# Two heads' matmuls issued in turn, and 512-column accumulators for z and the convolution, in a hybrid attention and state-space block

## The chip, the core and the metric

The kernel runs on one core of a Trainium2 chip. TensorE (PE) multiplies, its weight loads are listed apart (PEld); VectorE (DVE), ScalarE (ACT) and GpSimd (POOL) do the elementwise work, SyncE (SP) issues most transfers. Times are device microseconds (us) of one execution. Everything is float32; the large products run in float32r, a form that TensorE takes in one pass, and the small ones in plain float32, which stands in the trace as two weight loads and two matmuls for each matmul of the program.

## What is computed

A decoder block over 256 positions with 2048 channels: a modulated RMS norm, one wide input projection, a sparse attention branch and a Mamba-2 branch from it, a gated merge, and a SwiGLU feed-forward. Cut to the parts that the change touches:

```python
proj = h @ w_in
c_q, c_kv, k_idx, w_idx, z, xbc, dt_raw, g_a, g_b = jnp.split(proj, split_points, axis=-1)
...
# lightning indexer, 16 heads of 64, for two blocks of 128 queries
idx_score = jnp.einsum('bqh,bqhs->bqs', wi,
                       jax.nn.relu(jnp.einsum('bqhd,bsd->bqhs', qi, k_idx)))
...
# Mamba-2: depthwise convolution over 6144 channels, then chunks of 128 positions
conv = lax.conv_general_dilated(xbc, conv_w[:, None, :], ...)
conv = jax.nn.silu(conv + conv_b)
...
y_intra = jnp.einsum('btsgh,bsghp->btghp', w, xq)
y_inter = jnp.einsum('btgn,bghpn->btghp', cq, state) * jnp.exp(a_cs)[..., None]
...
y = y.reshape(B, L, D_INNER) * jax.nn.silu(z)
```

z has 4096 channels and xbc 6144.

## The kernel before

**Products in three terms.** Channels lie on the partitions, the 256 positions on the columns. Each weight tile of 128x128 is split into a rounded part wh (ACT, line 155) and a rest wl (DVE, line 156), and each moving operand is a 512-column tile: columns 0 to 255 its rounded part, 256 to 511 its rest. A product is wh times both halves plus wl times the rounded half. `mm3` (line 177) writes it in one of two forms, by the accumulator's width. With 256 columns it issues three matmuls of 256 columns (lines 182 to 184) into one sum. With 512 columns it issues one matmul of 512 columns (line 179) and one of 256 (line 180); then the two halves of the accumulator still have to be added, which `evac` (line 220) does: ACT copies the upper half to SBUF (line 223), DVE adds the lower half to it (line 224). A weight tile and what mm3 does with it is called a block below; a job is 16 blocks, one piece of 1 MB of weights.

**Who uses which.** Before the change the wide form is used by the projections pa, out, gu and dn, and the narrow form by the first part of the input projection (acc_s), by iq, by z (acc_z, 32 jobs), by the convolution's input (acc_cv, 48 jobs) and by pb. acc_s, acc_z, acc_cv and acc_gu have h as moving operand (gu's is a second tile h2 in the same place, with the same tag of a pool of one buffer); pb has y, pa has o, dn has ffact.

**What follows a z job.** `add_z` (line 686): ACT takes the tanh out of the accumulator (line 689), DVE forms (tanh + 1) times the accumulator (line 690), and the result goes to DRAM. **What follows a convolution job.** `conv_post` (line 811): ACT copies the accumulator to u (line 827) and makes the first tap from it (line 831), DVE adds three taps (line 833), ACT takes the tanh (834), DVE multiplies (836). After six such jobs `ssd_gen` runs the recurrence of one of eight groups, spread over the following jobs' blocks.

**The two-head matmuls.** In `ssd_gen` (lines 915 to 928) four tiles py of a group each take two heads, the first on output partitions 0 to 63, the second on 64 to 127. Each head has three float32 matmuls of 128 contraction rows, 64 output partitions and 128 columns (lines 922, 923, 924), so a py tile has six in the program and twelve in the trace. In `index_gen` (line 572) each of 16 heads has 64 contraction rows, even heads on partitions 0 to 63, odd ones on 64 to 127, each with its own accumulator; two matmuls a head (lines 580, 581).

**Order.** The kernel is written as a list of jobs. Their weights are loaded ahead on SP's queue, and a job's split is called two jobs before its matmuls (AHEAD = 2, three buffers each for wh and wl). What follows a product is deferred to the next job, and generators advance at set blocks of a job. Every engine takes its instructions in the order in which the framework's scheduler put them down; NACC = 4 accumulators are in turn.

Of the kernel before, what the change touches and what calls it, by code (L numbers as in the profile page):

```python
# [9 lines left out]
F32 = mybir.dt.float32  # L10
# [6 lines left out]
P = 128  # L17
# [26 lines left out]
def hybrid_block_kernel(  # L44
# [43 lines left out]
    def ps_side(name):  # L88
        return pss.tile([P, 512], F32, tag="ps", name=name)
# [326 lines left out]
    def full(key, src, post, **kw):  # L416
        product_jobs(key, [src], [(0, k) for k in range(KT)], hr, lambda m, acc: post(acc), **kw)
# [155 lines left out]
    def index_gen():  # L573
        t = A["t"]
        sc, kT, wi = A["sc"], A["kT"], A["wi"]
        for hd in range(NH):
            q = A["qi"][(hd % 2) * 64 : (hd % 2) * 64 + 64, hd // 2]
            kk = kT[(hd % 2) * 64 : (hd % 2) * 64 + 64]
            ps = ps_side(f"ix{hd}")
            pe.matmul(ps[:, 0:128], q[:, 0:128], kk[:, 0:128], start=True, stop=True)  # L580
            pe.matmul(ps[:, 128:384], q[:, 128:256], kk, start=True, stop=True)
# [104 lines left out]
    def add_z(j, ticks=1):  # L686
        def post(acc):
            th = tmp.tile([P, L], F32, tag="zt", name="zt")
            act.activation(th, acc, AF.Tanh, scale=0.5)
            dve.scalar_tensor_tensor(th, th, 1.0, acc, op0=ALU.add, op1=ALU.mult)  # L690
            nc.sync.dma_start(d_z[j], th)

        full(f"z{j}", w_z[j], post, ticks=ticks)
# [119 lines left out]
    def conv_post(g, i):  # L813
# [3 lines left out]
        def post(acc):  # L817
# [9 lines left out]
            act.activation(u[:, 3:], acc, AF.Copy)  # L827
# [3 lines left out]
            act.activation(c, acc, AF.Identity, scale=w(3), bias=cc[:, C_CB + j : C_CB + j + 1])  # L831
# [10 lines left out]
    def ssd_gen(g, xc, bc, ar):  # L842
# [72 lines left out]
        for j in range(4):  # L915
            z = load_z(j)
            py = ps_side("py")
            for i in range(2):
                hd = 2 * j + i
                o = py[64 * i : 64 * i + 64]  # L920
                xs = slice(64 * hd, 64 * hd + 64)
                pe.matmul(o[:, 0:128], xd[:, 0, xs], dd[:, hd, 0:128], start=True, stop=True)
                pe.matmul(o[:, 128:256], xd[:, 1, xs], dd[:, hd, 128:256], start=True, stop=False)
                pe.matmul(o[:, 128:256], st[:, xs], cd[:, hd], start=False, stop=True)
            if prev:
                finish(*prev)
            prev = (j, py, z)
            yield
# [21 lines left out]
    def add_conv(g, i, pre=None):  # L950
        full(f"cv{g}_{i}", w_ssm[6 * g + i], conv_post(g, i), pre=pre, ticks=3)
# [361 lines left out]
```

## Time and profile before

| | us |
|---|---|
| median of 3 runs | 2071.28 |
| lowest and highest | 2068.83, 2073.79 |
| the profiled execution, its own time | 2073.97 |
| its span, first to last instruction | 2072.0 |

The page says how long each engine was busy, and which chain of work ended last. Matmuls overlap in the trace (a matmul's record lasts some 280 ns while the next begins after 120), so PE's busy share hides small gaps; how fast PE goes is read from the starts of matmuls that follow each other.

### The profile page before, as it was taken

To read this page: it belongs to the slowest core of one execution; us is meant where nothing else is said; L and a number is where in the kernel's file an instruction comes from. 1 tells how busy PE (TensorE), PEld (TensorE's weight loads), DVE (VectorE), ACT (ScalarE), POOL (GpSimd) and SP (SyncE) were. 2 spreads that over 40 slices of the span, in tenths; PEclk is the share of its full clock that TensorE was granted. 3 is DMA by queue.
4 is the path that set the end of the run, shared out by engine and by line. 5 is a ranking of instruction groups with operands and counts; after the bars stand their busy time and mean duration, and the time that the engine had idled before them with its cause. 6 is when DMAs were issued, how large, how long until landed. Compare 5 with 4: busy or idle time off the path is not lost.

```text
span 2072.0 us, 34189 instructions
## 1 busy us (share of the span) xinstructions
PE 2003.7 (97%) x14116; PEld 1858.8 (90%) x14116; DVE 1462.3 (71%) x1779; ACT 1018.0 (49%) x1408; POOL 257.4 (12%) x216
## 2 busy tenths in 40 slices
PE   2999999999999999999999999999999999999997
PEld 2999999999899999999999978788888888888886
DVE  7799778866778887778777855667776555544443
ACT  3544654564354665566663444444444444443442
POOL 4043200310000111110112334000000000000000
PEclk9999999999999999999999999999999999999998
DMA  7888777666887766766565685457776555565552
GB/s 309 326 328 312 289 249 276 233 210 235 299 323 251 246 242 231 252 219 238 219 237 210 238 272 212 145 206 272 276 271 218 191 190 184 194 213 186 190 189 85
DMA packets 99468, 490.35 MB, mean 237 GB/s; under 512 B 10448, under 2 KB 43584, under 8 KB 44272
## 3 DMA queue, kind: packets, MB, share of 16 engines
q1 hardware_dynamic: 97648, 484.09, 65.1%
q0 software_dynamic: 704, 3.15, 0.5%
q8 instruction: 111, 1.82, 0.3%
q10 hardware_dynamic: 960, 0.92, 0.1%
q14 instruction: 45, 0.37, 0.0%
HBM read 473.35 MB, written 17.92 MB: 237 GB/s over the span
## 4 chain that ended last, share of the span: by engine, by line
PE 82%; issue 8%; DVE 6%; ACT 2%; DMA 1%; POOL 1%; DVEq 0%; SPq 0%; POOLq 0%; ACTq 0%
PE acc_gu L179 15%; PE acc_dn L179 8%; PE acc_gu L180 8%; PE acc_cv L182 4%; PE acc_cv L183 4%; PE acc_cv L184 4%; PE acc_dn L180 4%; PE acc_pa L179 3%; PE acc_out L179 3%; PE acc_pb L182 2%; PE acc_pb L183 2%; PE acc_pb L184 2%; PE acc_s L184 2%; PE acc_z L182 2%; PE acc_z L183 2%
## 5 line engine op out<-in xcount | busy, mean ns | idle before, releaser
L156 DVE TENSOR_TENSOR wl<-raw,wh 128x2048 fp32r<-128x2048 f32 (+1 forms) x329 | 754.5, 2294 | 363.8 <-ACT wh L155 362.5
L155 ACT ACTIVATE wh<-raw 128x2048 fp32r<-128x2048 f32 (+1 forms) x329 | 624.1, 1898 | 463.2 <-PE acc_dn L179 99.8
L179 PE MATMUL acc_gu<-h,wh 128*128 128x512 f32 x1312 | 463.9, 399 | 0.0
L180 PE MATMUL acc_gu<-h,wl 128*128 128x256 f32 x1312 | 368.5, 281 | 0.0
L179 PEld LDWEIGHTS acc_gu<-h,wh 128*128 128x128 f32 x1312 | 246.5, 188 | 61.5
L179 PE MATMUL acc_dn<-ffact,wh 128*128 128x512 f32 x704 | 248.8, 396 | 0.0
L180 PEld LDWEIGHTS acc_gu<-h,wl 128*128 128x128 f32 x1312 | 247.8, 189 | 0.0
L182 PE MATMUL acc_cv<-h,wh 128*128 128x256 f32 x768 | 223.1, 291 | 0.0
L183 PE MATMUL acc_cv<-h,wh 128*128 128x256 f32 x768 | 217.2, 283 | 0.0
L184 PE MATMUL acc_cv<-h,wl 128*128 128x256 f32 x768 | 217.1, 283 | 0.0
L180 PE MATMUL acc_dn<-ffact,wl 128*128 128x256 f32 x704 | 198.5, 282 | 0.0
L183 PE MATMUL acc_s<-h,wh 128*128 128x256 f32 x640 | 182.5, 286 | 1.3 <-DVE h L368 1.3
L182 PE MATMUL acc_s<-h,wh 128*128 128x256 f32 x640 | 182.5, 287 | 1.2 <-ACT h L366 1.2
L184 PE MATMUL acc_s<-h,wl 128*128 128x256 f32 x640 | 182.1, 286 | 1.4 <-DVE wl L156 1.4
L391 DVE SCALAR_TENSOR_TENSOR acc<-raw,cact,acc 128x1024 f32<-128x1024 f32 x120 | 159.0, 1325 | 6.7 <-DMA raw<-in_ada_dram 6.2
L179 PEld LDWEIGHTS acc_dn<-ffact,wh 128*128 128x128 f32 x704 | 132.3, 188 | 31.9
L182 PEld LDWEIGHTS acc_cv<-h,wh 128*128 128x128 f32 x768 | 146.9, 191 | 5.6 <-issue 5.3
L183 PEld LDWEIGHTS acc_cv<-h,wh 128*128 128x128 f32 x768 | 147.0, 191 | 1.0 <-issue 1.0
L182 PE MATMUL acc_z<-h,wh 128*128 128x256 f32 x512 | 147.2, 287 | 0.0
L184 PEld LDWEIGHTS acc_cv<-h,wl 128*128 128x128 f32 x768 | 147.0, 191 | 0.0
L182 PE MATMUL acc_pb<-y,wh 128*128 128x256 f32 x512 | 145.7, 285 | 0.0
L184 PE MATMUL acc_z<-h,wl 128*128 128x256 f32 x512 | 144.9, 283 | 0.0
(301 smaller groups left out, 4031.1 us busy)
## 6 DMA issues: line engine op xcount, KB each, us to landing
raw<-in_ada_dram SPq DMA_DIRECT2D x91, 1024.0 KB, 5.0
raw<-in_w_gu_dram SPq DMA_DIRECT2D x88, 1024.0 KB, 4.8
raw<-in_w_ssm_dram SPq DMA_DIRECT2D x48, 1024.0 KB, 4.9
raw<-in_w_dn_dram SPq DMA_DIRECT2D x44, 1024.0 KB, 4.8
raw<-in_w_s_dram SPq DMA_DIRECT2D x40, 1024.0 KB, 5.1
raw<-in_w_z_dram SPq DMA_DIRECT2D x32, 1024.0 KB, 5.1
raw<-in_w_pb_dram SPq DMA_DIRECT2D x32, 1024.0 KB, 4.8
raw<-in_w_pa_dram SPq DMA_DIRECT2D x16, 1024.0 KB, 5.3
```

What stands on the lines that cost most here:

```text
L155: act.activation(whf[:, o], raw[:, o], AF.Copy)
L156: dve.tensor_tensor(wlf[:, o], raw[:, o], whf[:, o].bitcast(F32), op=ALU.subtract)
L179: pe.matmul(acc, wh, rhs, start=first, stop=last)
L180: pe.matmul(acc[:, :L], wl, rhs[:, :L], start=False, stop=last, skip_group_check=True)
L182: pe.matmul(acc, wh, rhs[:, :L], start=first, stop=False)
L183: pe.matmul(acc, wh, rhs[:, L:], start=False, stop=False)
L184: pe.matmul(acc, wl, rhs[:, :L], start=False, stop=last)
L391: dve.scalar_tensor_tensor(a, r, cact[:, k : k + 1], a, op0=ALU.mult, op1=ALU.add)
```

## The change

- `add_z` and `add_conv` call for the wide form, so their 32 and 48 jobs issue lines 179 and 180 in place of 182 to 184. Their accumulators then need `evac`. For z it writes a new tile zs, from which tanh and the product are taken. For the convolution it writes u itself, in place of ACT's copy, and the first tap is made from u.
- py: the same six matmuls, but both heads' first, then both heads' second, then both heads' third.
- The index: two heads get their accumulators together; both heads' first matmul, then both heads' second.

The load of d_skip in contiguous form (`bias_gen`) is in both kernels alike. With the change the program has 1280 matmuls fewer, 80 DVE instructions and 32 ACT instructions more; SP's and POOL's lists have as many instructions as before.

```diff
         for hd in range(NH):
-            q = A["qi"][(hd % 2) * 64 : (hd % 2) * 64 + 64, hd // 2]
-            kk = kT[(hd % 2) * 64 : (hd % 2) * 64 + 64]
-            ps = ps_side(f"ix{hd}")
-            pe.matmul(ps[:, 0:128], q[:, 0:128], kk[:, 0:128], start=True, stop=True)
-            pe.matmul(ps[:, 128:384], q[:, 128:256], kk, start=True, stop=True)
+            if hd % 2 == 0:
+
+                rows_ = [slice(64 * i, 64 * i + 64) for i in range(2)]
+                pair = [ps_side(f"ix{hd + i}") for i in range(2)]
+                for o, r in zip(pair, rows_):
+                    pe.matmul(o[:, 0:128], A["qi"][r, hd // 2, 0:128], kT[r, 0:128], start=True, stop=True)
+                for o, r in zip(pair, rows_):
+                    pe.matmul(o[:, 128:384], A["qi"][r, hd // 2, 128:256], kT[r], start=True, stop=True)
+            ps = pair[hd % 2]
...
+            v = tmp.tile([P, L], F32, tag="zv", name="zs")
+            evac(acc, v)
             th = tmp.tile([P, L], F32, tag="zt", name="zt")
-            act.activation(th, acc, AF.Tanh, scale=0.5)
-            dve.scalar_tensor_tensor(th, th, 1.0, acc, op0=ALU.add, op1=ALU.mult)
+            act.activation(th, v, AF.Tanh, scale=0.5)
+            dve.scalar_tensor_tensor(th, th, 1.0, v, op0=ALU.add, op1=ALU.mult)
...
-        full(f"z{j}", w_z[j], post, ticks=ticks)
+        full(f"z{j}", w_z[j], post, ticks=ticks, wide=True)
...
-            act.activation(u[:, 3:], acc, AF.Copy)
+            evac(acc, u[:, 3:])
...
-            act.activation(c, acc, AF.Identity, scale=w(3), bias=cc[:, C_CB + j : C_CB + j + 1])
+            act.activation(c, u[:, 3:], AF.Identity, scale=w(3), bias=cc[:, C_CB + j : C_CB + j + 1])
...
-            for i in range(2):
-                hd = 2 * j + i
-                o = py[64 * i : 64 * i + 64]
-                xs = slice(64 * hd, 64 * hd + 64)
+
+            pair = [(py[64 * i : 64 * i + 64], 2 * j + i, slice(128 * j + 64 * i, 128 * j + 64 * i + 64)) for i in range(2)]
+            for o, hd, xs in pair:
                 pe.matmul(o[:, 0:128], xd[:, 0, xs], dd[:, hd, 0:128], start=True, stop=True)
+            for o, hd, xs in pair:
                 pe.matmul(o[:, 128:256], xd[:, 1, xs], dd[:, hd, 128:256], start=True, stop=False)
+            for o, hd, xs in pair:
                 pe.matmul(o[:, 128:256], st[:, xs], cd[:, hd], start=False, stop=True)
...
-        full(f"cv{g}_{i}", w_ssm[6 * g + i], conv_post(g, i), pre=pre, ticks=3)
+        full(f"cv{g}_{i}", w_ssm[6 * g + i], conv_post(g, i), pre=pre, ticks=3, wide=True)
```

PE's order at the first py tile, which stands between blocks of the convolution job cv1_2. Before:

```order
L182 MATMUL acc_cv_2_0_7303<-h,wh_7141 128x256
L183 MATMUL acc_cv_2_0_7303<-h,wh_7141 128x256
L184 MATMUL acc_cv_2_0_7303<-h,wl_7142 128x256
L922 MATMUL py<-ar,xd 64x128
L923 MATMUL py<-ar,xd 64x128
L924 MATMUL py<-cd,sta 64x128
L922 MATMUL py<-ar,xd 64x128
L923 MATMUL py<-ar,xd 64x128
L924 MATMUL py<-cd,sta 64x128
```

and after:

```order
L179 MATMUL acc_cv_2_0_6903<-h,wh_6767 128x512
L180 MATMUL acc_cv_2_0_6903<-h,wl_6768 128x256
L927 MATMUL py<-ar,xd 64x128 x2
L929 MATMUL py<-ar,xd 64x128 x2
L931 MATMUL py<-cd,sta 64x128 x2
```

A block of the convolution has two matmuls in place of three, and the heads of a py tile stand in turn (x2 is one for each head).

DVE's order at the job cv4_2, from the split of a later job's weights to the third tap. Before:

```order
L156 TENSOR_TENSOR wl_9520<-raw_9413,wh_9519 128x2048
L833 SCALAR_TENSOR_TENSOR cv<-u_6466,cc,cv 128x256
L907 SCALAR_TENSOR_TENSOR xc<-xc,dsk,py 128x256
L833 SCALAR_TENSOR_TENSOR cv<-u_6466,cc,cv 128x256
L391 SCALAR_TENSOR_TENSOR acc_1_0_9171<-raw_9517,cact,acc_1_0_9171 128x1024
L833 SCALAR_TENSOR_TENSOR cv<-u_6466,cc,cv 128x256
```

and after:

```order
L156 TENSOR_TENSOR wl_8758<-raw_8665,wh_8757 128x2048
L224 TENSOR_TENSOR u_6226<-acc_cv_2_0_8675,ev 128x256
L913 SCALAR_TENSOR_TENSOR xc<-xc,dsk,py 128x256
L391 SCALAR_TENSOR_TENSOR acc_1_0_8451<-raw_8755,cact,acc_1_0_8451 128x1024
L839 SCALAR_TENSOR_TENSOR cv<-u_6226,cc,cv 128x256
L391 SCALAR_TENSOR_TENSOR acc_1_0_8451<-raw_8755,cact,acc_1_0_8451 128x1024
L839 SCALAR_TENSOR_TENSOR cv<-u_6226,cc,cv 128x256 x2
```

The sum into u (line 224) is new and stands ahead of the taps, behind a split.

DVE's order ahead of the attention's first transposes pT, which wait for the scaled rows (line 719 before, 725 after; two heads, two pieces each). Before:

```order
L391 SCALAR_TENSOR_TENSOR acc_0_0_3312<-raw_4047,cact,acc_0_0_3312 128x1024
L713 TENSOR_SCALAR mx<-mx 128x2
L717 RECIPROCAL mx<-mx 128x2
L391 SCALAR_TENSOR_TENSOR acc_0_0_3312<-raw_4047,cact,acc_0_0_3312 128x1024
L719 TENSOR_SCALAR part<-part,mx 128x128
L156 TENSOR_TENSOR wl_4200<-raw_4128,wh_4199 128x2048
L719 TENSOR_SCALAR part<-part,mx 128x256
```

and after:

```order
L696 SCALAR_TENSOR_TENSOR zt<-zt,zs 128x256
L719 TENSOR_SCALAR mx<-mx 128x2
L391 SCALAR_TENSOR_TENSOR acc_0_0_3312<-raw_3951,cact,acc_0_0_3312 128x1024
L723 RECIPROCAL mx<-mx 128x2 x2
L391 SCALAR_TENSOR_TENSOR acc_0_0_3312<-raw_3951,cact,acc_0_0_3312 128x1024
L725 TENSOR_SCALAR part<-part,mx 128x128
L725 TENSOR_SCALAR part<-part,mx 128x256
L725 TENSOR_SCALAR part<-part,mx 128x128
L156 TENSOR_TENSOR wl_4092<-raw_4020,wh_4091 128x2048
L725 TENSOR_SCALAR part<-part,mx 128x256
```

Three of the four scaled pieces stand ahead of the split now, where one did; z's product (line 696) moved ahead of the two adaLN steps (line 391).

## Rows read from the trace of the kernel before

**Rows 1.** The page, parts 1 and 4: busy time and share of PE and DVE, and the chain of work that ended last, by engine.

```profile
PE 2003.7 (97%) x14116; PEld 1858.8 (90%) x14116; DVE 1462.3 (71%) x1779; ACT 1018.0 (49%) x1408; POOL 257.4 (12%) x216
...
PE 82%; issue 8%; DVE 6%; ACT 2%; DMA 1%; POOL 1%; DVEq 0%; SPq 0%; POOLq 0%; ACTq 0%
```

**Rows 2.** The groups of PE's instructions by form, of the whole span: line, engine, operation, tiles, shapes, count, then busy us and mean ns of one.

```profile
L182 PE MATMUL acc_cv<-h,wh 128*128 128x256 f32 x768 | 223.1, 291 | 0.0
...
L182 PE MATMUL acc_z<-h,wh 128*128 128x256 f32 x512 | 147.2, 287 | 0.0
...
L922 PE MATMUL py<-ar,xd 128*64 128x128 f32 x128 | 22.6, 298 | 0.0
```

**Rows 3.** PE in order of time (start us, length us, line, tiles, shapes): first and last row of five runs of blocks that nothing interrupts. z, 17 blocks apart; pa, 12 apart; the convolution, 18 apart; pb between convolution jobs, 12 apart; gu, 51 apart.

```profile
304.85 0.28 PE L182 MATMUL acc_z<-h,wh 128*128 128x256 f32 x1
...
310.97 0.28 PE L182 MATMUL acc_z<-h,wh 128*128 128x256 f32 x1
...
519.71 0.39 PE L179 MATMUL acc_pa<-o,wh 128*128 128x512 f32 x1
...
523.90 0.39 PE L179 MATMUL acc_pa<-o,wh 128*128 128x512 f32 x1
...
619.85 0.28 PE L182 MATMUL acc_cv<-h,wh 128*128 128x256 f32 x1
...
626.33 0.28 PE L182 MATMUL acc_cv<-h,wh 128*128 128x256 f32 x1
...
914.91 0.28 PE L182 MATMUL acc_pb<-y,wh 128*128 128x256 f32 x1
...
919.16 0.28 PE L182 MATMUL acc_pb<-y,wh 128*128 128x256 f32 x1
...
1621.95 0.40 PE L179 MATMUL acc_gu<-h,wh 128*128 128x512 f32 x1
...
1639.97 0.40 PE L179 MATMUL acc_gu<-h,wh 128*128 128x512 f32 x1
```

**Rows 4.** PE in order of time at the first py tile; a row with x2 merges two matmuls.

```profile
673.80 0.28 PE L184 MATMUL acc_cv<-h,wl 128*128 128x256 f32 x1
674.01 0.43 PE L922 MATMUL py<-ar,xd 128*64 128x128 f32 x2
674.28 0.27 PE L923 MATMUL py<-ar,xd 128*64 128x128 f32 x1
674.29 0.32 PE L922 MATMUL py<-ar,xd 128*64 128x128 f32 x1
674.39 0.27 PE L923 MATMUL py<-ar,xd 128*64 128x128 f32 x1
674.45 0.27 PE L922 MATMUL py<-ar,xd 128*64 128x128 f32 x1
...
674.78 0.38 PE L924 MATMUL py<-cd,sta 128*64 128x128 f32 x2
675.09 0.39 PE L182 MATMUL acc_cv<-h,wh 128*128 128x256 f32 x1
```

**Rows 5.** PE in order of time at two heads of the index; x4 merges the first matmuls of two heads, two passes each.

```profile
323.89 0.50 PE L580 MATMUL ix<-kT,part 64*128 64x128 f32 x4
```

**Rows 6.** What PE waited for between 300 and 1190 us: total us, times, longest.

```profile
PE pT L723 <- DVE part L719: 3.3, 3, 2.1
PE ynb L289 <- DVE rcol L271: 0.9, 2, 0.5
```

**Rows 7.** Busy time of each engine in stretches (us, then PE, PEld, DVE, ACT, POOL, granted clock as a share of full speed, DMA share, GB/s): DVE's fullest 20 us in the convolution stage, the whole of that stage, and the stretch of the index's top-k.

```profile
820.00:840.00 20.00, 20.00 (x169) 20.00 (x168) 19.05 (x25) 14.79 (x25) 0.00 (x0) 1.00 0.62 220
...
600.00:1090.00 490.00, 489.06 (x4110) 476.83 (x4109) 390.55 (x469) 304.16 (x477) 58.36 (x56) 1.00 0.67 242
...
360.00:380.00 20.00, 20.00 (x168) 19.90 (x168) 18.88 (x61) 8.89 (x16) 4.98 (x7) 1.00 0.47 166
```

**Rows 8.** Groups by form of DVE and ACT, 506 to 600 us, where pa uses evac: the split, the sum and the copy; mean ns of one behind the bar's comma.

```profile
L156 DVE TENSOR_TENSOR wl<-raw,wh 128x2048 fp32r<-128x2048 f32 x16 | 36.6, 2289 | 21.2 <-ACT wh L155 21.2
...
L224 DVE TENSOR_TENSOR sa<-acc_pa,ev 128x256 f32<-128x256 f32 x16 | 6.7, 420 | 2.2 <-ACT ev L223 1.8
...
L223 ACT ACTIVATE ev<-acc_pa 128x256 f32<-128x256 f32 x16 | 5.9, 368 | 10.8 <-PE acc_pa L180 10.8
```

**Rows 9.** The split that came closest to its use in the convolution stage, DVE in order of time, and the first matmul that reads that wl (found by counting sixteen such matmuls to a job).

```profile
1010.55 2.28 DVE L156 TENSOR_TENSOR wl<-raw,wh 128x2048 fp32r<-128x2048 f32 x1
...
1016.45 0.28 PE L184 MATMUL acc_cv<-h,wl 128*128 128x256 f32 x1
```

**Rows 10.** DVE in order of time ahead of the first pT, and PE there.

```profile
385.02 0.28 DVE L719 TENSOR_SCALAR part<-part,mx 128x128 f32<-128x128 f32 x1
385.21 2.28 DVE L156 TENSOR_TENSOR wl<-raw,wh 128x2048 fp32r<-128x2048 f32 x1
387.42 0.34 DVE L719 TENSOR_SCALAR part<-part,mx 128x256 f32<-128x256 f32 x1
...
384.14 0.28 PE L184 MATMUL acc_z<-h,wl 128*128 128x256 f32 x1
385.35 0.33 PE L723 MATMUL pT<-ident,part 128*128 128x128 f32 x1 [0.93 <-DVE part L719]
```

**Rows 11.** PE in a stretch just behind those transposes: busy time, granted clock, DMA share, GB/s.

```profile
390.00:391.00 1.00, 1.00 (x7) 0.50 0.97 410
```

## The prediction

> **What bounds the kernel now.** I read the page first: PE is busy 97% of the span and makes 82% of the chain that ended last [rows 1]. Then I looked at what PE waits for in the stretch that the change touches, 300 to 1190 us: two kinds of wait, 4.2 us together [rows 6]. So in this stretch PE's own pace is the time, and what an edit is worth is what it takes out of PE's stream of starts, as long as DVE and ACT still deliver the splits early enough. The reader is to look at starts, not at lengths: a narrow matmul's record is 0.28 us long, but the next begins 0.12 us later. A block's price is therefore the distance of equal rows divided by the blocks between them [rows 3]:
> - narrow, moving operand h: z (310.97 - 304.85)/17 = 0.3600 us, convolution (626.33 - 619.85)/18 = 0.3600 us;
> - narrow, another operand: pb (919.16 - 914.91)/12 = 0.3542 us, in the same stage as the convolution;
> - wide, operand h: gu (1639.97 - 1621.95)/51 = 0.3533 us;
> - wide, another operand: pa (523.90 - 519.71)/12 = 0.3492 us.
>
> **The wide form, z and convolution.** 512 z blocks and 768 convolution blocks [rows 2] go from three matmuls to two. The nearest row is gu: same form, and its operand lies where h lies. So 0.3600 - 0.3533 = 0.0067 us a block, times 1280 = **8.5 us** off PE's stream. Bounds: with pa's pace it would be 0.0108 x 1280 = 13.8 us. The low end comes from pb. Narrow pb is as fast as wide gu to 0.0009 us; if the 0.0058 us by which h is slower than y stayed with h whatever the form, only 0.0009 x 1280 = 1.2 us would be left. I take gu, since it is h in the wide form. The Trainium skill (TensorE: Matmul & The Clock Gate, section "Wait — 56ns, not 53.3ns?") gives a fixed cost of about 2.5 ns for each matmul at the full clock, over its columns; by that an estimate for one matmul less in a block is 2.5 ns, 3.2 us in all. The rows do not agree: they show 6.7 ns between the forms.
>
> **The py tiles.** 128 records of line 922 are 64 heads of two passes, so 32 tiles [rows 2]. A tile takes 675.09 - 673.80 = 1.29 us from the last block's start to the next one's [rows 4]. The first head's passes start at 674.01 and, in the same x2 row, soon after, then at .28 and .39; the second head's first starts only at 674.29, though it depends on nothing of the first head. From there on both heads run at once: starts of one lie between starts of the other (.39, .45). The tile ends with the second head's last pass, so what it loses is the late start, 0.28 us. In the program's order the whole first head stands ahead of the second. In turn, only two passes stand ahead of the second head's first; one pass takes 674.39 - 674.28 = 0.11 us, the shift that is left while both run is 674.45 - 674.39 = 0.06 us. With a shift between 0.06 and 0.11 us the tile saves 0.22 to 0.17 us; I take 0.20, times 32 = **6.4 us**. Bounds: nothing, if the second head still starts late; 0.28 x 32 = 9.0 us, if both start together, as the index's heads come near to doing: their four passes take 0.50 us to the end of the last record [rows 5], and a record of 128 columns lasts 0.27 us [rows 4], so four starts lie within 0.23 us, where passes of 0.11 us one behind another would need 0.33. The Trainium skill (same page, Part 3, section "The mechanism") says that weight loads overlap matmuls in flight only when the row groups differ; the two heads of py share all 128 rows. By that rule the order is worth nothing, a rival below. The trace speaks against it: second-head passes start between first-head passes at 674.39 and 674.45.
>
> **The index.** Its two heads already run at once before the change [rows 5], so turning them brings nothing: 0, with 0.3 us either way for the accumulators now being taken in twos.
>
> **What is added.** evac costs DVE 0.42 us and ACT 0.37 us [rows 8]. The convolution's ACT copy existed already, so ACT gets 32 x 0.37 = 12 us and DVE 80 x 0.42 = 34 us. None of it is on the path, if the splits stay early. In the convolution stage DVE is busy 390.6 of 490 us [rows 7]; 48 + 12 sums add 25 us: 416 of some 478 us, 87%. Its fullest 20 us have 19.05, and three or four sums add 1.5: DVE falls 0.5 us behind there. The cover is the split's lead: the closest in this stage ended at 1010.55 + 2.28 = 1012.83, and its wl was first read at 1016.45, 3.6 us later [rows 9]. ACT's first tap and z's tanh now wait for DVE's sum, which can stand behind a split of 2.29 us, and behind them on ACT stands the next rounding (line 155); that shifts a split by at most 2.29 + 0.42 = 2.7 us, under 3.6. So I cost it at nothing, and the order lists say that no transfer is added or moved to another queue.
>
> **The one place where DVE is ahead of PE in the path** is the first pT. PE reached it at 384.14 + 0.12 and waited 3.3 us [rows 6, 10]. Its inputs come from the top-k, which DVE begins when the last index heads are done and which fills 18.88 of 20 us [rows 7]. What z gains behind the index is lost here. In DVE's new order z's sum and z's product stand ahead of the scaling, 0.42 us more than before, while three pieces rather than one stand ahead of the split, so that fewer transposes are left behind it. I count a loss of **0.6 us**. This wait is followed by a stretch at the lower clock, 0.50 of full speed, that is 1.2 GHz [rows 11]. It may go or come again with the wait; I leave it as it is.
>
> **Sum.** -8.5 - 6.4 + 0 + 0.6 = -14.3 us. The profiled execution, 2073.97 us with 1.97 us around its span, becomes 2059.7. It lay 2.7 us over the median of 2071.28; against the median the forecast is **2057.0 us**.
>
> **Rivals.**
> 1. *The order of py is worth nothing* (each head's passes wait for the other head's weights as they stand). For it: the second head starts 0.28 us late though free. Against it: both heads then run at once [rows 4]. Time: 2071.3 - 8.5 + 0.6 = 2063.4.
> 2. *The wide form saves little*, since h, not the count of matmuls, makes z and the convolution slow. For it: pb at 0.3542 in the same stage. Against: gu at 0.3533 with h [rows 3]. Time: 2071.3 - 1.2 - 6.4 + 0.6 = 2064.3. With rival 1 as well: 2070.7.
> 3. *Slower: DVE's sums come into the path.* Place: z and convolution jobs, where rounding (ACT) waits behind a tap or tanh that waits for the sum on DVE, and the split behind that. It decides from the point where a split's delay passes its lead, 3.6 us at the closest [rows 9]; from then on each job pays the sum's 0.42 us on PE. All 80 jobs: 33.6 us, 2090.6, slower. Half of them: 16.8 us, 2073.8, no change that can be told. Against it: PE waits for no split in this stage now [rows 6], and DVE stays under 90%.
> 4. *The change doesn't do what it says*: the order lists show both edits as written, so this has no chance of its own.
>
> **How the numbers follow.** Forecast 0.72 (2057.0, its own range 2050 to 2062), rival 1 0.10, rival 2 0.07, both 0.03, rival 3 half 0.05 and whole 0.03. The range takes in rivals 1 and 2 on top and, below, pa's pace with most of the py bound (-13.8 - 9.0 + 0.6 would be 2049.1): 2049 to 2065.5. A measurement of this kernel tells some 0.2%, 4.1 us, from no change: faster holds the forecast, rivals 1 and 2: 0.89; same, below 2075.4 and above 2067.1, holds both rivals together and the half of rival 3: 0.08; slower 0.03.
>
> **What would show it.** Right: L179 rows of acc_z and acc_cv with blocks 0.353 us apart; py tiles of 1.06 to 1.12 us from block to block, with the second head's first pass at most 0.11 us behind the first head's; no new wait of PE for wl; the pT wait at 3 to 4.5 us. Wrong: blocks still at 0.359; py still at 1.29; PE waiting for wl or for accumulators between 600 and 1090 us; a second stretch at the lower clock in this part. A loss beyond these against the forecast would mean that a wait I hold covered is not.

## The result and the profile after

| | before | after |
|---|---|---|
| median, us | 2070.33 (5 runs, 2068.83 to 2073.79) | 2052.2 (5 runs, 2049.12 to 2060.75) |
| ratio | 1 | 0.9918, 95% interval 0.9893 to 0.9942 |
| profiled execution, its own time | 2073.97 | 2049.12 |
| its span | 2072.0 | 2047.4 |

The change takes 0.8% off, some 17 us. The spans of the two profiled executions differ by 24.6 us, so part of what they show is not the change; the experiments sort out most of it.

The page after, parts 1 and 4, as in [rows 1]:

```profile
PE 1978.9 (97%) x12836; PEld 1777.9 (87%) x12836; DVE 1482.4 (72%) x1859; ACT 1033.8 (50%) x1440; POOL 257.4 (13%) x216
...
PE 81%; issue 8%; DVE 6%; ACT 2%; DMA 2%; POOL 1%; DVEq 0%; SPq 0%; POOLq 0%; ACTq 0%
```

PE has 1280 matmuls fewer and still bounds the kernel. Its blocks, first and last row of stretches without a break, as in [rows 3]: z, 18 blocks apart; the convolution early in its stage, 22 apart, and late, 30 apart; gu early, 100 apart, and late, 100 apart.

```profile
304.68 0.39 PE L179 MATMUL acc_z<-h,wh 128*128 128x512 f32 x1
...
310.92 0.39 PE L179 MATMUL acc_z<-h,wh 128*128 128x512 f32 x1
...
618.90 0.40 PE L179 MATMUL acc_cv<-h,wh 128*128 128x512 f32 x1
...
626.53 0.40 PE L179 MATMUL acc_cv<-h,wh 128*128 128x512 f32 x1
...
932.58 0.40 PE L179 MATMUL acc_cv<-h,wh 128*128 128x512 f32 x1
...
943.18 0.40 PE L179 MATMUL acc_cv<-h,wh 128*128 128x512 f32 x1
...
1334.94 0.39 PE L179 MATMUL acc_gu<-h,wh 128*128 128x512 f32 x1
...
1369.60 0.39 PE L179 MATMUL acc_gu<-h,wh 128*128 128x512 f32 x1
...
1599.86 0.40 PE L179 MATMUL acc_gu<-h,wh 128*128 128x512 f32 x1
...
1635.19 0.40 PE L179 MATMUL acc_gu<-h,wh 128*128 128x512 f32 x1
```

Divide again. z: 6.24/18 = 0.3467 us. Convolution: 7.63/22 = 0.3468 and 10.60/30 = 0.3533. gu, which the change does not touch: 34.66/100 = 0.3466 and then 35.33/100 = 0.3533. So a wide block has two paces in one execution, 6.7 ns apart, and the prediction had measured gu at the slow one. The mean over all blocks without a break is 0.3496 us for z (0.3597 before) and 0.3504 for the convolution (0.3596 before). The trace of before held two paces already: pa, whose row the prediction took for the other operand's, went at 0.3490 us up to 540 us and slower behind the ada product that follows there. The rows are of before, 100 blocks apart, (578.47 - 543.14)/100 = 0.3533:

```profile
543.14 0.39 PE L179 MATMUL acc_pa<-o,wh 128*128 128x512 f32 x1
...
578.47 0.40 PE L179 MATMUL acc_pa<-o,wh 128*128 128x512 f32 x1
```

A py tile, as in [rows 4]; x4 merges two heads with two passes each:

```profile
671.76 0.28 PE L180 MATMUL acc_cv<-h,wl 128*128 128x256 f32 x1
671.97 0.44 PE L927 MATMUL py<-ar,xd 128*64 128x128 f32 x4
672.24 0.39 PE L929 MATMUL py<-ar,xd 128*64 128x128 f32 x4
672.46 0.39 PE L931 MATMUL py<-cd,sta 128*64 128x128 f32 x4
672.78 0.50 PE L179 MATMUL acc_cv<-h,wh 128*128 128x512 f32 x1
```

From block to block it is 672.78 - 671.76 = 1.02 us, where it was 1.29. In the trace's single records the second head's first pass starts 7 ns behind the first head's, and the twelve starts take 0.60 us (0.87 before). What PE waited for between 300 and 1190 us, as in [rows 6]:

```profile
PE pT L729 <- DVE part L725: 5.0, 3, 2.3
PE ada L395 <- DVE acc L391: 1.8, 2, 1.2
PE ynb L289 <- DVE rcol L271: 0.4, 2, 0.2
```

There is still no wait for a split (wl). The wait for pT grew from 3.3 to 5.0 us, a wait for an adaLN sum (ada) came, and ynb lost 0.5. The ada wait is 1.3 us in the second profile of the change (e4 below) and at most 0.4 in the traces of before, e1, e2, e3 and e5; what causes it was not tested. Busy time of the engines in the convolution stage, as in [rows 7] (its end is earlier now), in two windows at the first pT, as in [rows 11], and in one stretch within the convolution stage:

```profile
820.00:840.00 20.00, 20.00 (x122) 17.78 (x122) 19.59 (x24) 13.01 (x21) 1.04 (x1) 1.00 0.69 241
600.00:1075.00 475.00, 474.49 (x3162) 417.00 (x3161) 405.43 (x530) 312.85 (x488) 60.49 (x56) 1.00 0.69 251
...
386.00:389.00 3.00, 1.11 (x4) 0.71 (x4) 3.00 (x3) 1.15 (x2) 1.30 (x3) 0.50 0.92 328
390.00:392.00 2.00, 2.00 (x11) 2.00 (x11) 1.97 (x9) 1.50 (x6) 0.00 (x0) 0.50 0.72 205
...
809.30:812.50 3.20, 3.20 (x12) 2.72 (x12) 3.20 (x5) 2.37 (x6) 0.00 (x0) 0.50 0.43 161
```

The last row is what the prediction called a sign of being wrong: a second stretch at the lower clock between 600 and 1090 us. PE was busy all through it and ahead of it (two yn and eight ada matmuls stand just ahead). In it the convolution's blocks are 0.64 us apart:

```profile
809.94 0.63 PE L179 MATMUL acc_cv<-h,wh 128*128 128x512 f32 x1
...
810.58 0.63 PE L179 MATMUL acc_cv<-h,wh 128*128 128x512 f32 x1
```

Five such blocks in place of five at 0.35 make an estimate of 1.5 us for the stretch. The traces of before, e2, e3 and e5 have none in this stage, e1 has one, e4 two; why was not tested.

In the convolution stage DVE (third figure) is at 405 of 475 us, 85%, and PE still at 474.5 of 475. The closest split now ends 2.0 us ahead of its first use (in e4 1.0), where the closest before ended 3.6 us ahead [rows 9]:

```profile
622.84 2.29 DVE L156 TENSOR_TENSOR wl<-raw,wh 128x2048 fp32r<-128x2048 f32 x1 [2.13 <-ACT wh L155]
...
627.11 0.27 PE L180 MATMUL acc_z<-h,wl 128*128 128x256 f32 x1
```

It is not the same split: this job's had a lead of 4.9 us before. Counted from the convolution's first matmul it ends 1.9 us later (2.9 in e4), and its first use comes 1.1 us earlier.

The first pT, DVE and then PE in order of time, as in [rows 10]:

```profile
380.67 1.01 DVE L696 SCALAR_TENSOR_TENSOR zt<-zt,zs 128x256 f32<-128x256 f32 x1
...
385.03 1.67 DVE L725 TENSOR_SCALAR part<-part,mx 128x128 f32<-128x128 f32 x3
386.62 2.83 DVE L156 TENSOR_TENSOR wl<-raw,wh 128x2048 fp32r<-128x2048 f32 x1
389.37 0.34 DVE L725 TENSOR_SCALAR part<-part,mx 128x256 f32<-128x256 f32 x1
...
385.60 0.33 PE L729 MATMUL pT<-ident,part 128*128 128x128 f32 x1 [2.29 <-DVE part L725]
386.36 0.90 PE L729 MATMUL pT<-ident,part 128*128 128x128 f32 x3 [0.43 <-DVE part L725]
389.77 0.69 PE L729 MATMUL pT<-ident,part 128*128 128x128 f32 x2 [2.30 <-DVE part L725]
```

DVE begins the scaling at 385.03, within 0.01 us of when it did before, although PE is 1.1 us ahead there (its wait begins at 385.60 - 2.29 = 383.31; before at 385.35 - 0.93 = 384.42); z's product (line 696) stands ahead of it. The last piece waits behind a split that took 2.83 us here (2.28 before), so the last two transposes start at 389.77 and 390.04, where they did at 388.74 and 389.01 before. The granted clock is 0.50 (1.2 GHz) in both windows above, at 386 as at 390 us; PE waited in part of the first. Before it was still full there and fell only later:

```profile
386.00:388.60 2.60, 0.56 (x3) 0.32 (x3) 2.50 (x7) 0.64 (x2) 0.00 (x0) 1.00 0.95 315
```

By the granted clock the stretch at 0.50 lasts from 388.7 to 392.1 us before and from 385.9 to 392.7 after.

### The profile page after: what moved, and what is told of

Read it like the earlier page. It is cut to its first block, busy times and chain, and to the rows that moved or that the text cites. A ratio compares the mean times of both kernels' runs of the same rounds, so it can differ in the third digit from the quotient of the medians.

```text
span 2047.4 us, 31779 instructions
## 1 busy us (share of the span) xinstructions
PE 1978.9 (97%) x12836; PEld 1777.9 (87%) x12836; DVE 1482.4 (72%) x1859; ACT 1033.8 (50%) x1440; POOL 257.4 (13%) x216
## 4 chain that ended last, share of the span: by engine, by line
PE 81%; issue 8%; DVE 6%; ACT 2%; DMA 2%; POOL 1%; DVEq 0%; SPq 0%; POOLq 0%; ACTq 0%
PE acc_gu L179 15%; PE acc_cv L179 8%; PE acc_dn L179 8%; PE acc_gu L180 8%; PE acc_dn L180 4%; PE acc_cv L180 4%; PE acc_z L179 4%; PE acc_out L179 3%; PE acc_s L184 3%; PE acc_s L183 3%; PE acc_s L182 3%; PE acc_pa L179 2%; PE acc_pb L182 2%; PE acc_pb L183 2%; PE acc_pb L184 2%
## 5 line engine op out<-in xcount | busy, mean ns | idle before, releaser
L179 PE MATMUL acc_cv<-h,wh 128*128 128x512 f32 x768 | 279.0, 405 | 0.0
L179 PE MATMUL acc_z<-h,wh 128*128 128x512 f32 x512 | 183.2, 400 | 0.0
L179 PEld LDWEIGHTS acc_cv<-h,wh 128*128 128x128 f32 x768 | 144.9, 189 | 37.8 <-issue 4.7
L182 PE MATMUL acc_pb<-y,wh 128*128 128x256 f32 x512 | 146.5, 286 | 0.0
L183 PE MATMUL acc_pb<-y,wh 128*128 128x256 f32 x512 | 143.9, 281 | 0.0
L184 PE MATMUL acc_pb<-y,wl 128*128 128x256 f32 x512 | 143.8, 281 | 0.0
```

Source lines behind the costliest of these rows:

```text
L179: pe.matmul(acc, wh, rhs, start=first, stop=last)
L182: pe.matmul(acc, wh, rhs[:, :L], start=first, stop=False)
L183: pe.matmul(acc, wh, rhs[:, L:], start=False, stop=False)
L184: pe.matmul(acc, wl, rhs[:, :L], start=False, stop=last)
```

## The experiments

Lengths of stretches, worked out from the starts of matmuls in the traces, in us (the convolution stage goes from its first matmul to its last):

| | before | after | py alone | wide alone | index alone | all, second run | narrow z first |
|---|---|---|---|---|---|---|---|
| first z job to last av | 199.3 | 198.3 | 198.9 | 199.9 | 199.3 | 199.1 | 197.9 |
| convolution stage | 488.6 | 472.6 | 483.9 | 478.7 | 488.6 | 475.0 | 473.0 |
| rest of pb, out | 217.8 | 213.7 | 215.8 | 217.0 | 217.9 | 214.7 | 213.2 |
| gu to dn | 467.2 | 462.9 | 462.9 | 464.6 | 467.2 | 467.2 | 467.2 |

The first four kernels ran on one chip, beside the kernel before: 2071.33 us, 20 runs from 2064.84 to 2075.76.

**e1: py alone.** The kernel before with the change's py part only:

```diff
-            for i in range(2):
...
+            for o, hd, xs in pair:
                 pe.matmul(o[:, 0:128], xd[:, 0, xs], dd[:, hd, 0:128], start=True, stop=True)
+            for o, hd, xs in pair:
                 pe.matmul(o[:, 128:256], xd[:, 1, xs], dd[:, hd, 128:256], start=True, stop=False)
+            for o, hd, xs in pair:
                 pe.matmul(o[:, 128:256], st[:, xs], cd[:, hd], start=False, stop=True)
```

> Only the order inside the py tiles is changed; z, the convolution and the index are as before. Theory (parts add up, each by what it takes out of TensorE's stream): a tile goes from 1.283 to about 1.016 us as in the changed kernel, 32 x 0.267 = 8.5 us less, 2062 us against 2070.3. Rival (the gain of the changed kernel came from elsewhere, the tiles' time was hidden): within 2 us of before. Blocks of gu: theory A says their pace has nothing to do with the change and comes out anywhere between 0.350 and 0.3535 us; the rival, that the wide form in the earlier stages moved it, says 0.3535 here.

Measured 2061.59 us (7 runs), ratio 0.996 (0.9942 to 0.9977), so 8.3 us. A tile takes 1.015 us where it took 1.283 (mean of the 32): 0.268 x 32 = 8.6 us. So the order of py alone makes the kernel faster, and the tiles' time was not hidden. That the two numbers are so close is in part luck: in the profiled execution the convolution stage, with 28 of the tiles, is 4.7 us shorter and not 28 x 0.268 = 7.5. A stretch at 0.50 of the clock (814.1 to 817.5 us) stands in it, and ynb waits 1.0 us longer there. And 4.3 us of this execution's gain came from gu, which went at 0.3467 us and then at 0.3533, as in the profile after, here without the wide form.

**e2: the wide form alone.**

```diff
-        full(f"z{j}", w_z[j], post, ticks=ticks)
+        full(f"z{j}", w_z[j], post, ticks=ticks, wide=True)
...
-        full(f"cv{g}_{i}", w_ssm[6 * g + i], conv_post(g, i), pre=pre, ticks=3)
+        full(f"cv{g}_{i}", w_ssm[6 * g + i], conv_post(g, i), pre=pre, ticks=3, wide=True)
```

with evac in both, as in the change.

> Only z and the convolution use 512-column accumulators; py and index in the order of before. Theory: 1280 blocks at 0.350 instead of 0.360 us, at most 12.8 us, less what the first pT wait gives back (about 2 us): 10 to 11 us, 2060 us. Rival 2 of the prediction (the operand h makes the blocks slow, not the form): 1 to 2 us, 2069. Rival 3 (DVE's sums come into the path): slower than 2066, with TensorE waiting for wl. Blocks of gu: 0.350 here if the wide form earlier is what moved it; anywhere between 0.350 and 0.3535 if not.

Measured 2061.56 us (8 runs), ratio 0.9956 (0.9941 to 0.997), so 9.1 us. The convolution stage, with 48 + 12 of the 80 jobs, is 9.9 us shorter, and 960 blocks x 0.0096 are 9.2. The stretch with the other 20 jobs is not shorter but 0.6 us longer: PE's pT wait is 4.9 us here, and the stretch at 0.50 of the clock is the longest of these traces, 385.7 to 396.0 us. gu was 2.6 us shorter in this profile.

**e3: the index alone.**

```diff
-            ps = ps_side(f"ix{hd}")
-            pe.matmul(ps[:, 0:128], q[:, 0:128], kk[:, 0:128], start=True, stop=True)
-            pe.matmul(ps[:, 128:384], q[:, 128:256], kk, start=True, stop=True)
+                for o, r in zip(pair, rows_):
+                    pe.matmul(o[:, 0:128], A["qi"][r, hd // 2, 0:128], kT[r, 0:128], start=True, stop=True)
+                for o, r in zip(pair, rows_):
+                    pe.matmul(o[:, 128:384], A["qi"][r, hd // 2, 128:256], kT[r], start=True, stop=True)
```

> Only the index's heads are issued in turn. Theory: the heads ran at once before, so nothing: 2070.3 within 1 us, seven stretches of index matmuls as long as before (2.24 us the first, 1.07 the others). Rival (taking accumulators in twos delays or frees something): a first stretch longer or shorter than 2.24 us by over 0.3 us and a time off by over 2 us. If the pace of gu and the length of the out stage vary here against the profile of before, they are not the change's doing.

Measured 2071.23 us (12 runs), ratio 1.0003 (0.9992 to 1.0015): no change, to 2 or 3 us. The seven stretches of index matmuls are as long as before.

**e4: the whole change again, beside the parts.** No edit.

> The changed kernel once more, with a second profile. Theory A (part of the 24.6 us between the two profiled executions belongs to stages that the change doesn't touch and varies from one execution to the next): the median stays near 2052 us, and in the new profile the out stage, 6.4 us shorter in the first profile, or gu, 4.3 us shorter, comes out different by 2 us or more, while z and the convolution stages keep their lengths within 1 us. Rival (the change shortened out and gu by shifting when transfers land): both come out as in the first profile within 1 us.

Measured 2052.52 us (6 runs), ratio 0.9921 (0.9903 to 0.9939), 16.4 us. The parts add up: 8.3 + 9.1 - 0.6 = 16.8, each with 2 to 4 us on either side. gu went at 0.3533 us all through here and at two paces in the profile after, so gu's 4.3 us between the first two profiles do not belong to every execution of the change. Whether the change makes the fast start of gu more frequent is open: the three profiles that have neither the wide form nor py in turn (before, e3, e5) show gu slow all through, in six of the nine others where no cut stands ahead of gu it begins at 0.3467. If it does, up to 4.3 us of the gain in an execution come that way. The convolution stage is 2.4 us longer than in the first profile of the change, where the expectation allowed 1; two stretches at 0.50 of the clock stand in it here (654.4 to 657.8 and 978.7 to 982.1 us), one there.

**e5: why the second head of py started late.** The kernel before, with four passes ahead of the second head instead of six:

```diff
-            for i in range(2):
...
+            for step, i in ((0, 0), (1, 0), (0, 1), (2, 0), (1, 1), (2, 1)):
+                o, hd, xs = pair[i]
```

> The kernel before, with one edit: py's six matmuls in the order A1 B1... that is first head's 1st, first head's 2nd, second head's 1st, first head's 3rd, second head's 2nd, second head's 3rd (each is two passes in the trace). So four passes stand ahead of the second head's first pass, where the kernel before has six and the changed kernel two. Theory 1 (PE starts a pass out of turn only if few enough queued passes stand ahead of it, as for the index, where four stood ahead in the kernel before and its two heads ran at once): the second head starts within 0.02 us of the first and a tile takes 1.02 to 1.07 us. Theory 2 (only a strict turn lets the heads run at once): the second head starts behind the first head's first two matmuls, 0.12 to 0.2 us late, and a tile takes 1.12 to 1.22 us. Theory 3 (nothing but the exact turn helps): 0.28 us late, 1.28 us a tile.

One run, 2069.38 us; the trace decides. PE in order of time at one tile:

```profile
988.35 0.28 PE L184 MATMUL acc_cv<-h,wl 128*128 128x256 f32 x1
988.56 0.45 PE L922 MATMUL py<-ar,xd 128*64 128x128 f32 x4
988.83 0.44 PE L924 MATMUL py<-ar,xd 128*64 128x128 f32 x4
989.05 0.44 PE L926 MATMUL py<-cd,sta 128*64 128x128 f32 x4
989.41 0.38 PE L182 MATMUL acc_cv<-h,wh 128*128 128x256 f32 x1
```

The tile takes 1.06 us, and the first rows of both heads merge into one x4: the single records have the second head 14 ns behind the first. Theory 1 holds. A strict turn isn't needed for the early start, though its tiles are 0.05 us shorter still: with two or four passes ahead the second head starts at once, with six it starts 0.28 us late, that is when the first head's third pass starts, with four not yet done. It runs past passes that stand ahead of it in the program: for PE the order of the list is not always the order of the starts.

**e6: are the sums covered?** The changed kernel with each convolution sum made twice:

```diff
             evac(acc, u[:, 3:])
+            evac(acc, u[:, 3:])
```

> The changed kernel, with evac called twice for each of the convolution's 48 accumulators (the same sum written again to the same place): 48 x 0.42 = 20 us more DVE and 48 x 0.37 = 18 us more ACT in the convolution stage, and the first tap stands behind it. Theory (the sums are covered by the split's lead, some 3.6 us at the closest): time as the changed kernel's within 3 us, 2049 to 2055, and PE waits for no wl between 600 and 1090 us beyond 0.5 us in all. Rival (DVE's sums come into the path once DVE is near full, 420 + 20 of 475 us): each job pays 0.42 us or more, so 2062 for half of the jobs and 2072 for all, with PE waits for wl at lines 179 or 180.

Measured 2059.36 us (4 runs), ratio 0.9936 (0.9918 to 0.9954), beside a kernel before of 2072.47 (11 runs, the same chip for e5 to e8). That lies between the theory's 2055 and the rival's 2062, and the interval overlaps those of the changed kernel, so the trace has to tell. The convolution stage is 481.0 us long, where it is 472.6 and 475.0 in the two profiles of the change. What PE waited for, 300 to 1190 us:

```profile
PE yn L278 <- POOL ysqa L919: 5.2, 5, 1.5
PE pT L729 <- DVE part L725: 4.8, 3, 2.5
```

Still no wait for wl (the closest lead is 2.4 us), so the split's lead covers even twice the sums. The new wait is another one: yn, the norm's matmul at the end of a group's recurrence, whose input POOL adds up from what DVE, POOL and ACT make of py. The changed kernel has no such wait in its two profiles. So in this one trace of doubled sums the cover gives out first at yn, and not where the prediction looked; which step delays POOL was not followed.

**e7: the ten z jobs ahead of the first pT stay narrow.** In the changed kernel:

```diff
+            v = acc
+            if j >= 10:
+                v = tmp.tile([P, L], F32, tag="zv", name="zs")
+                evac(acc, v)
...
-        full(f"z{j}", w_z[j], post, ticks=ticks, wide=True)
+        full(f"z{j}", w_z[j], post, ticks=ticks, wide=j >= 10)
```

> The changed kernel, but the ten z jobs ahead of the first pT stay narrow, as in the kernel before. Theory 1 (what the wide form gains ahead of the first pT is only waited for there, since pT's inputs come from DVE's top-k): PE reaches pT about 1 us later, its wait for line 725's kind of scaling falls from 5.0 to 3.3 or 4 us, and the whole time is that of the changed kernel within 2 us, 2050 to 2054. Theory 2 (the wait is longer because z's sums on DVE delay the scaling, and a longer stretch at 1.2 GHz follows it): pT comes earlier, the wait is under 3.4 us and the time falls by 2 to 4 us, to 2048 to 2050. Theory 3 (the gain is kept): the time rises by 10 x 16 x 0.0098 = 1.6 us.

Measured 2053.38 us (6 runs), ratio 0.9899 (0.9884 to 0.9915). PE's waits, 300 to 600 us:

```profile
PE pT L731 <- DVE part L727: 3.3, 3, 2.1
```

Theory 3 falls: counted from the first z job PE comes 1.35 us later than in the profile after, and the stretch to the last av is 197.9 us, shorter than in any kernel with these jobs wide (198.3, 199.1, 199.9). e11 and e12 below, narrow there too, have 198.0 each; e6, e8, e9 and e10, wide, have 198.4 to 199.3. Between theories 1 and 2 the time doesn't decide, since the intervals of e4 and e7 overlap, and a wait of 3.3 us fits both. The traces show parts of both: the first pT starts 83.7 us behind the first z job, as in the profile after, but the last of its six transposes 0.9 us earlier. And the stretch at 0.50 of the clock lasts 3.4 us in all seven traces with these jobs narrow (before, e1, e3, e5, e7, e11, e12), 6.8 in six of the seven with them wide and 10.3 in the seventh, e2. The stretch to the last av, 0.4 to 2.0 us shorter, speaks for a small gain.

**e8: what changes the pace of a wide block.** The changed kernel, with eight plain float32 matmuls of one column ahead of 41 products of gu:

```diff
+    def cut():
+        ps = ps_side("cut")
+        for k in range(8):
+            pe.matmul(ps[:, k : k + 1], ones, cact[:, k : k + 1], start=True, stop=True)
```

> The changed kernel with eight extra matmuls of one column ahead of each of the 41 later gu products (their result is not used), shaped as the ada products that cut into the stream now. It costs 41 x 1.8 = 74 us or less; the time isn't the point, the pace of gu's blocks is. Theory (the distance of wide blocks takes one of a few values, 346.7, 350.0 or 353.3 ns, and it is drawn anew where other matmuls cut into the stream): gu's blocks show at least two of these values, each constant between two cuts. Rival (the value belongs to the execution or to the stage): one value through all of gu, or one change only. Rival 2 (a cut always leads to the slow value): 353.3 ns after every cut.

One run, 2123.02 us. The 41 stretches between cuts went at 353.3, 346.7, 353.3, 346.7 ns and so on in turn. The turn was out of step only at the two cuts that stood beside an ada product, which cut into the stream too. The theory holds, and more strictly than expected: a cut turned the pace over each time.

**e9: does the cut's size matter?**

```diff
+    sizes = [8] * 2 + [1] * 4 + [2] * 4 + [3] * 4 + [4] * 4 + [5] * 2 + [6] * 2 + [7] * 2
+    sizes = [(n, False) for n in sizes] + [(n, True) for n in [1] * 5 + [2] * 4 + [3] * 4 + [4] * 4]
```

> The changed kernel, with extra matmuls (result not used) ahead of each of the 41 later gu products, of different sizes: 2 cuts of eight plain float32 matmuls of one column, then four cuts each of one, two, three and four, two each of five, six and seven, then cuts in one-pass float32r of 128 columns, five of one, four each of two, three and four; and one plain matmul ahead of every second product of dn. Only the pace of the blocks behind each cut is looked at. Theory 1 (every cut turns the pace over, whatever its size, since the state is one of two and a break in the stream flips it): 353.3 and 346.7 alternate through all of gu, as with eight. Theory 2 (the state follows the number of matmuls or weight loads between, odd or even): some sizes flip and the others leave the pace as it is. Theory 3 (the pace behind a cut is set by how long the cut is, not by the pace ahead of it): a size always leads to the same pace. dn's pace, 353.3 in every run so far, goes to 346.7 at some cut by theories 1 and 2, and stays if dn's operand has one pace only.

One run. PE in order of time around the first cut of two (four records), 30 blocks ahead of it and 30 behind:

```profile
1387.25 0.40 PE L179 MATMUL acc_gu<-h,wh 128*128 128x512 f32 x1
...
1397.85 0.40 PE L179 MATMUL acc_gu<-h,wh 128*128 128x512 f32 x1
1398.20 0.50 PE L1100 MATMUL cut<-cact,ones 128*128 128x1 f32 x4
...
1398.99 0.40 PE L179 MATMUL acc_gu<-h,wh 128*128 128x512 f32 x1
...
1409.39 0.40 PE L179 MATMUL acc_gu<-h,wh 128*128 128x512 f32 x1
```

10.60/30 = 0.3533 us ahead, 10.40/30 = 0.3467 behind. All 12 cuts of an even number of plain matmuls turned the pace, in both directions; all 12 of an odd number left 353.3 as it was (346.7 never stood ahead of an odd one). One cut of each kind stood right behind an ada product. The 17 one-pass cuts turned it in some places and not in others, without a rule that I could read. That is theory 2 for these plain matmuls. Their number is not the whole rule: an ada product has eight plain matmuls of one column itself, and in the twelve traces without a cut at every product it left 353.3 as it was in all 14 places and turned 346.7 in six of ten. dn, cut only by single matmuls, stayed at 353.3.

**e10 and e11: can the pace be had?** In every run without cuts gu went at 353.3 ns behind the last ada product. e10 is the changed kernel with two cuts; e11 has the narrow z of e7 as well:

```diff
-            lambda k: Fd["h2"][:, k], gu_post, wide=True,
+            lambda k: Fd["h2"][:, k], gu_post, wide=True, pre=cut if i == 24 else None,
...
             nc.sync.dma_start(Fd["x2"][:, m], d_x1[m])
+            if m == 1:
+                cut()
```

> The changed kernel with two plain float32 matmuls of one column (result not used, 0.4 us) ahead of gu product 24, which follows the last ada product, and again at the second product of dn. Theory (from 1571 us on gu went at 353.3 ns in every run without cuts, and two, four, six or eight plain matmuls turned 353.3 to 346.7): the 640 gu blocks behind the first cut go at 346.7 ns, which takes 640 x 6.67 = 4.3 us off; if dn's pace turns as well, its 660 remaining blocks give 4.4 us more. Time 2048.5 with gu alone, 2045 with both. Rival 1 (the turn shows in a profile, but the time is made elsewhere, so that it is given back): 2052. Rival 2 (the pace does not turn outside a series of cuts): 353.3 behind the cut and 2053.

> As the run before, and the ten z jobs ahead of the first pT stay narrow. Theory (their gain is given back at the first pT, and a shorter wait there means a shorter stretch at 1.2 GHz): 0 to 2 us under the run with two cuts, a pT wait of 3.3 us, 2043 to 2047. Rival (the wide form keeps its gain there): 1.6 us above the run with two cuts.

Measured 2050.79 us (6 runs, 2044.97 to 2053.77), ratio 0.9896 (0.9877 to 0.9915), and 2047.66 (4 runs, 2046.93 to 2049.4), ratio 0.989 (0.9873 to 0.9906); the kernel before had 2070.86 (11 runs). e10's interval overlaps the changed kernel's (e4), so its time alone shows no gain. In both traces the first cut turned gu from 353.3 to 346.7. The second did harm: dn began at 349.0 ns behind the fast gu and went at 353.3 behind its cut. So e10 kept one gain of two and gave away what dn had got; e11 against e10 is within their intervals.

**e12: the same without the second cut.**

```diff
-            if m == 1:
-                cut()
```

> As the run before without the second cut: the changed kernel, the ten z jobs ahead of the first pT narrow, and one cut of two plain matmuls ahead of gu product 24. In the last two profiles dn began at 349.0 ns a block and went to 353.3 behind the cut inside it. Theory (the pace holds until something cuts into the stream, so dn keeps 349.0 to its end): 658 x 4.3 ns = 2.8 us and the cut's 0.4 us off, 2044.5, ratio to the kernel before 0.987 to 0.9885. Rival (dn falls to 353.3 by itself at some later product): 2047 to 2048.

Measured 2044.65 us (4 runs, 2040.81 to 2045.59), ratio 0.9863 (0.9839 to 0.9886), the kernel before 2073.88 (7 runs). PE in order of time: 30 blocks ahead of the cut, the cut, 638 blocks of gu behind it, 700 of dn.

```profile
1550.03 0.40 PE L179 MATMUL acc_gu<-h,wh 128*128 128x512 f32 x1
...
1560.63 0.40 PE L179 MATMUL acc_gu<-h,wh 128*128 128x512 f32 x1
1560.98 0.50 PE L1098 MATMUL cut<-cact,ones 128*128 128x1 f32 x4
...
1561.77 0.40 PE L179 MATMUL acc_gu<-h,wh 128*128 128x512 f32 x1
...
1782.94 0.40 PE L179 MATMUL acc_gu<-h,wh 128*128 128x512 f32 x1
...
1784.34 0.40 PE L179 MATMUL acc_dn<-ffact,wh 128*128 128x512 f32 x1
...
2028.57 0.39 PE L179 MATMUL acc_dn<-ffact,wh 128*128 128x512 f32 x1
```

0.3533 ahead; 221.17/638 = 0.3467 in gu and 244.23/700 = 0.3489 in dn behind. 640 x 6.7 ns and 704 x 4.4 ns are 7.4 us, for 0.4 us of matmuls that compute nothing. This kernel beats both: its interval lies below the changed kernel's 0.9893 to 0.9942 (0.9903 to 0.9939 in e4). How much of that is the cut and how much the narrow z jobs, the times do not separate; no kernel has the one cut alone.

## Why the prediction was right

The forecast was 14.3 us off the kernel before; the two comparisons gave 0.0082 x 2071 = 17.0 and 0.0079 x 2071 = 16.4. The mechanism was the one named: the two edits took time out of PE's stream of starts, each by itself (e1, e2). The sizes, by the steps of the sum:

- **The wide form, forecast 8.5 us.** By the means of the blocks 0.0101 x 512 + 0.0092 x 768 = 12.2 us. The term was too small because gu, the row it was taken from, has two paces and showed only the slow one in the trace of before; it is between gu's value and the bound by pa's pace. That bound was read as the other operand's, though pa showed two paces in that trace. One matmul less in a block was worth 6.7 to 13.3 ns, not the 2.5 ns by the Trainium skill's fixed cost (TensorE: Matmul & The Clock Gate, "Wait — 56ns, not 53.3ns?"). Rival 2 is out.
- **py, forecast 6.4 us, measured 8.6 in the tiles.** The step that was wrong is the shift of 0.06 to 0.11 us: both heads start within 7 ns, as the index's do. The text had that case as its bound, 9.0. Rival 1 is out by e1, and with it, here, the Trainium skill's rule that weight loads overlap matmuls in flight only in other row groups (TensorE: Matmul & The Clock Gate, Part 3, "The mechanism"): the heads share all 128 rows, and their twelve passes start within 0.60 us.
- **The index, forecast 0 ± 0.3, measured 0.6 ± 2.4** (e3).
- **The sums, forecast at no cost.** No wait for wl in the profile after (0.4 us once in e4, at the first z block), with the closest lead down to 2.0 us and 1.0 in e4. Rival 3 did not come in; e6 shows that it would begin elsewhere, at yn. But the reason given was not sound: it allowed for a split 2.7 us later and left out that a faster PE uses it earlier. Leads shrank by up to 3.5 and 4.5 us in the two profiles, which the closest, 3.6, would not have stood in e4; the splits whose leads shrank most had 4.9 and 7.4 us. That they did was luck. And whether the ada wait of 1.8 and 1.3 us is a cost of the sums was not tested.
- **The first pT, forecast a loss of 0.6 us.** Too small. The 20 z jobs ahead of the convolution should give 20 x 16 x 0.0101 = 3.2 us; the stretch to the last av got 1.0 us shorter (0.3 in e4), so 2.2 to 2.9 us were lost there. What was missed: in e2, e4 and after the clock stayed at 0.50 for longer than before (6.8 or 10.3 us, not 3.4), where the forecast left it as it was, and DVE's last scaled piece came later, behind a split of 2.83 us. The wait of 3.3 us that the prediction took for one is three, of 0.9, 2.1 and 0.2 us. e7 shows that keeping these jobs narrow brings wait and stretch back; how the loss divides between clock and DVE was not measured.
- **The clock in the convolution stage, left as it was.** One stretch at 0.50 came in the profile after and two in e4, at an estimate of 1.5 us each.

By these, 12.2 + 8.6 - 2.2 to 2.9 = 17.9 to 18.6 us, less 1.5 or 3.0 for the clock in the convolution stage and 1.3 to 1.8 for ada; the ratios give 17.0 and 16.4, with 4 to 5 us on either side. The convolution stage alone, with 960 blocks and 28 tiles, should give 16.6 us less the clock's 1.5 and 3.0, that is 15.1 and 13.6; it gave 16.0 and 13.6.

So the total came within 3 us of the forecast partly because errors cancelled: both gains were put too small, by 3.7 and 2.2 us, and the losses too, by 3 us or more. Three of the prediction's own marks were missed: the pT wait (4.6 and 5.0 us, not 3 to 4.5), the tiles (1.02 us, not 1.06 to 1.12) and the second stretch at the lower clock.

## What to carry to other kernels

Price a block by the distance of its starts, and take it at several places of a trace: one stage of the same form can have two paces, and a term sized at one of them can be off by nearly half. Matmuls that can run at once on two halves of the array need not stand strictly in turn, but the second half's first must not stand behind too many of the first's (here four passes did no harm to its start, six did). Gains that lie ahead of another engine's chain are waited for at its end: keep them where PE sets the time.

## What the hardware showed unexpectedly

- A wide block takes 0.3467 or 0.3533 us, and keeps its pace for hundreds of blocks until other matmuls cut into the stream. In this kernel cuts of two, four, six or eight plain float32 matmuls turned it over (e8, e9), an odd number left the slow pace as it was, and so did the ada products, which have eight. An execution can begin gu in either: 0.3467 in the profile after, 0.3533 in e4, from the same program. Why is open; so is whether a single cut helps a kernel with other products around it. In e10 a cut made dn slower, 0.3490 to 0.3533.
- The narrow form takes 0.3600 us with h in every trace, and about 0.3535 with other operands, with y in part of pb in the profile after 0.3400; why h is slower was not tried.
- A pass of the second head starts ahead of passes that stand before it in the program, if four or fewer of them are left (e5). The Trainium skill (TensorE: Matmul & The Clock Gate, "Step-by-step: what each phase is for") has matmuls in program order and only weight loads ahead; the measured starts, 14 ns and 0.28 us, differ from that, and they decide.
